# Gate phase of a hybrid GLA/SSD/PEER layer: part of the gate scaling on ScalarE, copies of the selection one step later, and another order of the last scalings

## The chip, the cores and the metric

One core of one Trainium2 chip runs the whole layer. The metric is the device time of one execution in microseconds (us), taken as the median over runs.

## The reference

The layer takes 512 tokens of width 1024. It normalises them, mixes them with a gated linear attention and a state-space mixer (the first 260 us, untouched here), and then applies a mixture of single-neuron experts. Only this last part matters:

```python
def peer_ffn(xn, w_query, sub_keys, u, v):   # T=512 tokens, H=8 heads, K=16, 128 keys
    q = (xt @ w_query).reshape(T, H, 2, PEER_HALF)
    s = jnp.einsum('thpd,hpkd->thpk', q, sub_keys)
    top_s, top_i = lax.top_k(s, K)
    cand_s = top_s[:, :, 0, :, None] + top_s[:, :, 1, None, :]     # 16 x 16 sums
    best_s, best_pos = lax.top_k(cand_s.reshape(T, H, K * K), K)
    expert_idx = i1 * 128 + i2        # the two key indices at best_pos
    gate = jax.nn.softmax(best_s, axis=-1)
    ...
    hid = gelu(xt . u[expert_idx]) * gate          # 128 experts per token
    return sum over the 128 of hid * v[expert_idx]
# y = rmsnorm(h + peer_ffn(rmsnorm(h)))
```

## The kernel before

For three of the four blocks of 128 tokens (384 tokens, TD) the kernel does not gather experts: it computes gelu(x . u) for all 16384 experts in 128 tiles of 128 experts, multiplies by a dense matrix of gates (zero where an expert was not picked), and multiplies by all of v. The fourth block is done by gathering rows with indirect DMAs, one expert per token at a time, spread over the rest of the program. The instructions of each engine run in the order in which the code issues them; there is no scheduler. The stages, in time:

- Queries, scores and top-16 searches, until 387 us. VectorE does the searches.
- Selection, 387 to 464 us. `select(t)` finds, for the block t, the two key indices of each of the 128 picks with long 16-bit VectorE operations on a tile `gat`. It reads copies of the index lists (tile `k`) that ScalarE writes; `ties(t)` queues four such copies (`piece`), and two of them are issued in each following U step. There are two buffers `k`, so those of block 2 take the one that `select(0)` reads. Meanwhile TensorE does U steps (`u_run`): a U step makes one tile of x . u in 8 parts (`u_part`) of 3 matmuls each. Every four parts need one half of a tile of u, split by ScalarE into a high part `uh` and by GpSimd, in this stage, into the low part `ul`. `spread` and `spread2` transpose the picks and write the key indices `i1s`, `i2s` and the gates `gs` (high part `gs[:, 0]`, low part `gs[:, 1]`, 16 bit).
- The gate phase, 464 to 655 us, is a loop over 48 units of 8 tokens. `gprep(u + 1)` builds on VectorE, for the next unit, the one-hot matrix `A` of the second key, the one-hot `eq` of the first key, and `B`, which is `eq` times the high gate part (`B[:, 0]`) and times the low one (`B[:, 1]`), 1024 elements per partition each. TensorE multiplies A and B of the unit (16 matmuls to `pg`). ScalarE writes the results of experts whose U tile is not there yet to `ring` and `stage`; VectorE multiplies the others into `ring`. `A` and `B` have two buffers, `eq` has one. Between two units TensorE does 5 or 6 parts of a U step. In this phase `ul` is done by VectorE. After a whole U step `keep` issues two gelu operations on ScalarE (`ring<-pm` and `gl<-pm`); the product with `gl` follows on VectorE in the next unit.
- The V stage, 660 to 1474 us: v streams through, TensorE is busy throughout.
- `final()`: the last products, residuals, means and scalings of the output.

The units' order of issue is short:

```python
act(stage[0][:, :, ...], p3[:, RS:, :], AF.Copy)   # gunit(u), ScalarE
gprep(u + 1)
release()                                          # product with gl
tt(ring[:, :n, w], p3[:, :n, :], ring[:, :n, w], OP.mult)
...
gunit(u)                                           # the loop over units
while done * NU < parts * (u + 1):
    u_part(done % 8)                               # uh and ul at parts 0 and 4
    done += 1
```

There are `parts` = 8 * (59 - 2 - 26) = 248 parts for 48 units, so 40 units have 5 and 8 have 6. Each unit's parts hold one or two uh copies (62 in all, at parts 0 and 4 of each U step) and 31 times the end of a U step with its gelu pair. Counted from this arithmetic: 11 units issue one uh copy alone, 6 one copy and then the gelu pair, 17 the gelu pair and then one copy, 6 two copies, 7 a copy, the pair and a copy, 1 the pair and then two copies.

Of the kernel before, what the change touches and what calls it, by code (L numbers as in the profile page):

```python
# [7 lines left out]
F32 = mybir.dt.float32  # L8
# [6 lines left out]
AF = mybir.ActivationFunctionType  # L15
OP = mybir.AluOpType
# [9 lines left out]
TD = GT * 128  # L26
# [3 lines left out]
def bc(ap, axis, n):  # L30
    shape = list(ap.shape)
    shape.insert(axis, n)
    ix = tuple([slice(None)] * axis + [None])
    return ap[ix].to_broadcast(shape)
# [29 lines left out]
class Layer:  # L64
# [25 lines left out]
    def act(self, out, in_, f, **k):  # L90
        return self.S.activation(out, in_, f, **k)  # L91
# [4 lines left out]
    def tt(self, out, x, y, op):  # L96
        return self.V.tensor_tensor(out, x, y, op=op)  # L97

    def stt(self, out, x, s, y, op0, op1, **k):
        return self.V.scalar_tensor_tensor(out, x, s, y, op0=op0, op1=op1, **k)  # L100
# [767 lines left out]
    def experts(self):  # L868
        tc, nc, a, V, T, G = self.tc, self.nc, self.a, self.V, self.T, self.G
        act, tt, stt, load = self.act, self.tt, self.stt, self.load  # L870
        ident, nh, nl = self.ident, self.nh, self.nl
        ctx = ExitStack()
        c = ctx.enter_context(tc.tile_pool(name="ex", bufs=1, reuse_waits="tile"))
# [3 lines left out]
        def pt():  # L877
            return self.ps.tile([128, 512], F32, name="pm", tag="pm", bufs=self.nbank)
# [9 lines left out]
        UT = 8  # L888
# [83 lines left out]
        def ties(t):  # L972
            x = (kp if t % 2 else self.kr).tile([128, 2, 8, 16, 16], F16, name="k8", tag="k8", bufs=1)
            for e in range(2):
                for g in (slice(0, 4), slice(4, 8)):
                    pieces.append((t, x[:, e, g], bc(tif[:, t, g, e, :], 3, 16)))
            TIE[t] = x
# [4 lines left out]
        def piece():  # L982
            t, o, i = pieces.pop(0)
            act(o, i, AF.Copy)

        def select(t):

            while any(p[0] == t for p in pieces):
                piece()
            ii = kp.tile([128, 2, 8, 16], F32, name="ii", bufs=2)  # L990
            for e in range(2):
                oh = c.tile([128, 8, 16, 16], F16, name="gat", tag="gat", bufs=3)
                tt(oh, bc(CF[0][:, e, t], 2, 16), bc(itj if e else its, 1, 8), OP.is_equal if e else OP.is_ge)
                tt(oh, oh, TIE[t][:, e], OP.mult)
                for n in (8, 4, 2):
                    tt(oh[:, :, 0:n, :], oh[:, :, 0:n, :], oh[:, :, n:2 * n, :], OP.add)
                tt(ii[:, e], oh[:, :, 0, :], oh[:, :, 1, :], OP.add)
            IX[t] = ii
# [9 lines left out]
        def gates2():  # L1008
            sm = kp.tile([128, 2, NT, 8], F32, name="sm")
            V.tensor_reduce(sm[:, 0], bs, axis=AX.X, op=OP.add)  # L1010
            V.reciprocal(sm[:, 1], sm[:, 0])
            tt(bs, bs, bc(sm[:, 1], 3, 16), OP.mult)
# [2 lines left out]
        i1s = c.tile([128, TD], F16, name="i1s")  # L1015
        i2s = c.tile([128, TD], F16, name="i2s")
        gs = c.tile([128, 2, TD], F16, name="gs")
        SC = float(2 ** 14)
        flat = lambda x: x.rearrange("p h k -> p (h k)")

# [2 lines left out]
        def spread(t):  # L1023
            ii, g = IX.pop(t), bs[:, t]
            p = pt()
            T.transpose(p[:, 0:128], flat(ii[:, 0]), ident)
            T.transpose(p[:, 128:256], flat(ii[:, 1]), ident)
            T.transpose(p[:, 256:384], flat(g), ident)
            act(gs[:, 0, t * 128:(t + 1) * 128], p[:, 256:384], AF.Copy, scale=SC)
            SPR[t] = p  # L1030

        def spread2(t):
            p = SPR.pop(t)
            s = slice(t * 128, (t + 1) * 128)
            V.tensor_copy(i2s[:, s], p[:, 128:256])
            V.tensor_copy(i1s[:, s], p[:, 0:128])
            stt(gs[:, 1, s], p[:, 256:384], SC, gs[:, 0, s], OP.mult, OP.subtract)

        nu, gtok = [NPU], [0]
        held, hold = [], [False]  # L1040
# [19 lines left out]
        def u_part(i, pool=False):  # L1060
            e = nu[0]
            if e >= NE:
                return
            if i == 0:
                up[0] = pt()
            self.rhs_part(up[0][:, :TD], tsd, not hold[0] and nu[0] < RS - 4)
            if i in PP and pieces:
                piece()
            if i == 7:
                keep(e, up[0])  # L1070
                nu[0] += 1

        def u_run(n):
            for _ in range(n):
                for i in range(8):
                    u_part(i)
# [23 lines left out]
        gates1()  # L1100
        select(0)
        gates2()
        u_run(2)
        ties(2)
        u_run(1)
        select(1)
        u_run(2)
        spread(0)
        ties(3)
        select(2)  # L1110
        u_run(2)
        spread(1)
        u_run(1)
        spread2(0)
        spread2(1)
        select(3)
        u_run(2)
        spread(2)
        u_run(5)
# [52 lines left out]
        def gprep(u):  # L1172

            if u >= NU:
                return
            w = slice(u * UT, u * UT + UT)
            two = lambda x: bc(x.rearrange("p (a t) -> p a t", t=2), 2, 128)
            A = gp.tile([128, UT // 2, 128, 2], F16, name="A", bufs=2)
            eq = gp.tile([128, UT // 2, 128, 2], F16, name="eq")
            B = gp.tile([128, 2, UT // 2, 128, 2], F16, name="B", bufs=2)  # L1180
            tt(A, bc(itx, 1, UT // 2), two(i2s[:, w]), OP.is_equal)
            tt(eq, bc(itx, 1, UT // 2), two(i1s[:, w]), OP.is_equal)
            for i in range(2):
                tt(B[:, i], eq, two(gs[:, i, w]), OP.mult)
            AB[u] = A, B

        def gunit(u):
# [76 lines left out]
        def final():  # L1264

            nv = lambda: c.tile([128, 4], F32, name="rs3", bufs=4)
            hf = [slice(0, 512), slice(512, 1024)]
            junk = [c.tile([128, D], F32, name="gat", tag="gat", bufs=3), vp.tile([128, D], F32, name=f"vr{NE % 4}", bufs=1)]
            v = [nv() for _ in range(4)]

            def products(t):
                s = slice(t * 128, t * 128 + 128)
                for n in range(2):
                    for e in (NE - 2, NE - 1):
                        self.mm3(pv[t][n], HT[e][0][:, s], HT[e][1][:, s], *vs.parts[2 * e + n], False, e == NE - 1)

            def residual(t, n):
                h = hs[t][:, hf[n]]
                stt(h, pv[t][n], 1.0 / SC, h, OP.mult, OP.add)
                square(t, n)  # L1280

            def square(t, n):
                act(junk[t % 2][:, hf[n]], hs[t][:, hf[n]], AF.Square, accum_out=v[t][:, n:n + 1])

            def weight(t, n, eng):
                eng.tensor_tensor(hs[t][:, hf[n]], hs[t][:, hf[n]], wf[:, hf[n]], op=OP.mult)

            def mean(t):
                V.tensor_scalar(v[t][:, 2:3], v[t][:, 0:1], EPS * D, None, op0=OP.add)
                V.tensor_scalar(v[t][:, 0:1], v[t][:, 1:2], v[t][:, 2:3], 1.0 / D, op0=OP.add, op1=OP.mult)  # L1290

            def power(t):
                G.tensor_tensor(v[t][:, 3:4], v[t][:, 0:1], self.mhalf, op=OP.pow)

            def scale(t, cols=slice(0, D)):
                stt(hs[t][:, cols], hs[t][:, cols], v[t][:, 3:4], wf[:, cols], OP.mult, OP.mult)

            square(3, 0)
            square(3, 1)
            mean(3)  # L1300
            power(3)
            for t in range(3):
                products(t)
            residual(0, 0)
            residual(0, 1)
            scale(3)
            load(self.out[3], hs[3])
            mean(0)
            power(0)
            residual(1, 0)  # L1310
            weight(1, 0, G)
            scale(0, hf[0])
            residual(1, 1)
            residual(2, 0)
            scale(0, hf[1])
            load(self.out[0], hs[0])
            residual(2, 1)
            mean(1)
            power(1)
            scale(1, hf[1])  # L1320
            mean(2)
            power(2)
            act(hs[1][:, hf[0]], hs[1][:, hf[0]], AF.Copy, scale=v[1][:, 3:4])
            load(self.out[1], hs[1])
            weight(2, 0, V)
            act(hs[2][:, hf[0]], hs[2][:, hf[0]], AF.Copy, scale=v[2][:, 3:4])
            self.S.dma_start(self.out[2][:, hf[0]], hs[2][:, hf[0]])
            scale(2, hf[1])
            load(self.out[2][:, hf[1]], hs[2][:, hf[1]])
# [152 lines left out]
```

## Time and profile before

| | |
|---|---|
| median of 3 runs (lowest to highest) | 1491.26 us (1488.55 to 1494.8) |
| profiled execution | 1490.63 us |
| its span of instructions | 1488.9 us, the rest (1.7 us) lies around it |
| busy, TensorE / VectorE / ScalarE / GpSimd | 98% / 79% / 43% / 31% of the span |
| chain that ended last | TensorE 79%, VectorE 14%, issue 3%, ScalarE 2%, DMA 2% |

The busy shares are averages over stages with different limits. The chain that ended last, read in order of time, tells which engine sets the pace where: VectorE all through the selection, TensorE and VectorE in turn in the gate phase, TensorE in the V stage. A busy TensorE is modelled from its matmuls, so a small gap there can hide.

### The profile page before, as it was taken

What the parts mean: (1) busy time and instruction counts of PE and PEld (TensorE: products, weight loads), DVE (VectorE), ACT (ScalarE), POOL (GpSimd) and SP (SyncE); (2) the same over time, 40 slices, a digit from 0 to 9 for tenths busy, and PEclk for the clock granted to TensorE, in tenths of its full rate; (3) what the DMA queues carried; (4) which work ended last, traced back from release to release, by engine and by line L of the source; (5) the groups of instructions that cost most, each with busy time, mean ns of one, the idle gap of its engine ahead of it and who ended that gap; (6) DMA issues with size and microseconds to landing.
All of it is one profiled execution on the core that took longest, in us unless ns stands there. A gap on an engine that the chain in (4) does not pass through costs nothing.

```text
span 1488.9 us, 22403 instructions
## 1 busy us (share of the span) xinstructions
PE 1453.5 (98%) x7896; PEld 1276.4 (86%) x7896; DVE 1174.1 (79%) x2476; ACT 636.2 (43%) x1208; POOL 456.2 (31%) x383
## 2 busy tenths in 40 slices
PE   7999999999999999999999999999999999999997
PEld 6787778888989998889999999999999998888886
DVE  6542664789999999988778778777788888888886
ACT  6335743433654544443333333333333333444444
POOL 2002404444574000003333333333333334333331
PEclk9999999999999999999999999999999999999999
DMA  5231224222334556679998898889898888888894
GB/s 190 85 127 58 71 72 156 89 91 91 100 114 158 145 157 167 180 226 341 321 322 311 307 328 310 312 315 324 309 346 306 310 300 289 293 302 294 299 326 171
DMA packets 148883, 335.56 MB, mean 225 GB/s; under 512 B 64657, under 2 KB 73889, under 8 KB 148641
## 3 DMA queue, kind: packets, MB, share of 16 engines
q1 hardware_dynamic: 58672, 186.06, 36.8%
q0 software_dynamic: 36864, 134.23, 25.1%
q10 hardware_dynamic: 53232, 13.83, 4.0%
q8 instruction: 62, 1.02, 0.3%
q14 instruction: 53, 0.43, 0.1%
HBM read 315.79 MB, written 18.28 MB: 224 GB/s over the span
## 4 chain that ended last, share of the span: by engine, by line
PE 79%; DVE 14%; issue 3%; ACT 2%; DMA 2%; POOL 0%; DVEq 0%; POOLq 0%; SPq 0%; ACTq 0%
PE pm L109 25%; PE pm L108 25%; PE pm L110 25%; DVE gat L97 4%; DVE B L97 1%; PE pg L1196 1%; DVE ul L104 1%; ACT b L91 1%; DVE eq L97 1%; DVE A L97 1%; DVE ring L97 1%; DMA ur<-in_uT 1%; PE pm L914 1%; ACT tp L91 0%; PE pm L275 0%
## 5 line engine op out<-in xcount | busy, mean ns | idle before, releaser
L108 PE MATMUL pm<-nT,uh 128*128 128x384 f32 (+1 forms) x1152 | 401.7, 349 | 0.9 <-ACT nT L91 0.5
L110 PE MATMUL pm<-nT,ul 128*128 128x384 f32 (+1 forms) x1152 | 396.6, 344 | 3.0 <-POOL ul L104 3.0
L109 PE MATMUL pm<-nT,uh 128*128 128x384 f32 (+1 forms) x1152 | 396.4, 344 | 0.5 <-DVE nT L97 0.5
L109 PE MATMUL pm<-vl,hh 128*128 128x512 f32 x765 | 300.6, 393 | 0.2 <-DVE vl L104 0.2
L110 PE MATMUL pm<-vh,hl 128*128 128x512 f32 x765 | 300.5, 393 | 0.0
L108 PE MATMUL pm<-vh,hh 128*128 128x512 f32 x765 | 298.9, 391 | 0.2 <-ACT vh L91 0.2
L1145 POOL DMA_INDIRECT gat<-in_u,idx x128 | 137.9, 1078 | 455.3 <-DVE gat L100 449.5
L91 ACT ACTIVATE uh<-ur 128x512 fp32r<-128x512 f32 x288 | 180.6, 629 | 201.0 <-PE pm L109 180.9
L108 PEld LDWEIGHTS pm<-nT,uh 128*128 128x128 f32 x1152 | 217.7, 189 | 25.6 <-ACT uh L91 1.0
L109 PEld LDWEIGHTS pm<-nT,uh 128*128 128x128 f32 x1152 | 217.6, 189 | 24.8 <-DVE nT L97 1.1
L110 PEld LDWEIGHTS pm<-nT,ul 128*128 128x128 f32 x1152 | 217.5, 189 | 10.5 <-POOL ul L104 4.7
L1145 POOL DMA_INDIRECT gat<-in_v,idx x128 | 146.9, 1148 | 253.4 <-DVE n2a L100 209.6
L91 ACT ACTIVATE vh<-vr 128x512 fp32r<-128x512 f32 x255 | 159.4, 626 | 136.8 <-PE pm L110 134.0
L104 DVE TENSOR_TENSOR vl<-vr,vh 128x512 fp32r<-128x512 f32 x255 | 175.0, 687 | 35.0 <-ACT vh L91 34.4
L104 DVE TENSOR_TENSOR ul<-ur,uh 128x512 fp32r<-128x512 f32 x202 | 138.1, 688 | 48.8 <-ACT uh L91 48.4
L100 DVE SCALAR_TENSOR_TENSOR n2a<-gat,dots,n2a 128x1024 f32<-128x1024 f32 x128 | 163.8, 1280 | 14.8 <-DMA gat<-in_v,idx 10.8
L110 PEld LDWEIGHTS pm<-vh,hl 128*128 128x128 f32 x765 | 143.7, 188 | 30.4
L100 DVE SCALAR_TENSOR_TENSOR gat<-gat,n2a 128x1024 f32<-128x1024 f32 x128 | 156.0, 1219 | 9.5 <-DMA gat<-in_u,idx 9.2
L108 PEld LDWEIGHTS pm<-vh,hh 128*128 128x128 f32 x765 | 143.9, 188 | 14.2 <-ACT vh L91 0.7
L109 PEld LDWEIGHTS pm<-vl,hh 128*128 128x128 f32 x765 | 143.9, 188 | 14.2 <-DVE vl L104 0.5
L104 POOL TENSOR_TENSOR ul<-ur,uh 128x512 fp32r<-128x512 f32 x86 | 124.9, 1461 | 98.6 <-ACT uh L91 95.7
L91 ACT ACTIVATE gl<-pm 128x384 f32<-128x384 f32 (+15 forms) x102 | 45.4, 445 | 220.1 <-PE pm L110 220.1
(252 smaller groups left out, 1694.5 us busy)
## 6 DMA issues: line engine op xcount, KB each, us to landing
ur<-in_uT SPq DMA_DIRECT2D x128, 512.0 KB, 5.7
vr<-in_v SPq DMA_DIRECT2D x128, 512.0 KB, 5.3
gd<-stage ACTq DMA_DIRECT2D x6, 2208.0 KB, 14.0
ring<-gd SPq DMA_DIRECT2D x69, 192.0 KB, 5.4
wraw<-in_w_in SPq DMA_DIRECT2D x23, 512.0 KB, 4.3
ur<-in_w_query SPq DMA_DIRECT2D x16, 512.0 KB, 3.7
b<-in_x SPq DMA_DIRECT2D x8, 512.0 KB, 3.6
wraw<-in_w_out SPq DMA_DIRECT2D x8, 512.0 KB, 3.9
```

The lines of the kernel that those rows point to most:

```text
L91: return self.S.activation(out, in_, f, **k)
L97: return self.V.tensor_tensor(out, x, y, op=op)
L100: return self.V.scalar_tensor_tensor(out, x, s, y, op0=op0, op1=op1, **k)
L104: (self.G if pool else self.V).tensor_tensor(lo, src, hi.bitcast(F32), op=OP.subtract)
L108: T.matmul(out, lhi, rhi, start=start, stop=False)
L109: T.matmul(out, lhi, rlo, start=False, stop=False)
L110: T.matmul(out, llo, rhi, start=False, stop=stop)
L914: T.matmul(p[:, t * 128:(t + 1) * 128], q[:, t * 128:(t + 1) * 128], skT[:, b, :], start=True, stop=True)
L1145: G.indirect_dma_start(out=r, out_offset=None, in_=src, in_offset=bass.IndirectOffsetOnAxis(ap=idx[:, k:k + 1], axis=0))
L1196: T.matmul(o, A[:, t // 2, :, t % 2], B[:, i, t // 2, :, t % 2], start=i == 0, stop=i == 1)
```

## The change

Three edits come together. In the gate phase, the product of `eq` and the low gate part is split: VectorE keeps the first four tokens of a unit (512 elements), and ScalarE does the other four, one ACTIVATE of 128 elements for each token, with the token's low gate as a scale read from memory. For this the low parts are also kept in 32 bits (`gl32`), so `spread2` writes them there and copies them to `gs`. In the selection the `ties` of blocks 2 and 3 are queued one U step later, and `spread`, `select` and `spread2` change places a little. In `final()` the product of the last block's first half with the norm's weights moves to GpSimd, and the mean and power of the last block stand ahead of the second half's scaling of the block before.

```diff
+        gl32 = c.tile([128, TD], F32, name="gl32")
...
-            stt(gs[:, 1, s], p[:, 256:384], SC, gs[:, 0, s], OP.mult, OP.subtract)
+            stt(gl32[:, s], p[:, 256:384], SC, gs[:, 0, s], OP.mult, OP.subtract)
+            V.tensor_copy(gs[:, 1, s], gl32[:, s])
...
         gates2()
-        u_run(2)
+        u_run(3)
         ties(2)
-        u_run(1)
         select(1)
         u_run(2)
         spread(0)
+        select(2)
+        u_run(1)
         ties(3)
-        select(2)
         u_run(2)
         spread(1)
-        u_run(1)
         spread2(0)
+        select(3)
         spread2(1)
-        select(3)
         u_run(2)
...
             tt(eq, bc(itx, 1, UT // 2), two(i1s[:, w]), OP.is_equal)
-            for i in range(2):
-                tt(B[:, i], eq, two(gs[:, i, w]), OP.mult)
+            tt(B[:, 0], eq, two(gs[:, 0, w]), OP.mult)
+            k = UT // 4
+            tt(B[:, 1, :k], eq[:, :k], two(gs[:, 1, w.start:w.start + UT // 2]), OP.mult)
+
+            for t in range(UT // 2, UT):
+                act(B[:, 1, t // 2, :, t % 2], eq[:, t // 2, :, t % 2], AF.Copy, scale=gl32[:, w.start + t:w.start + t + 1])
...
             residual(2, 0)
+            weight(2, 0, G)
             scale(0, hf[1])
             load(self.out[0], hs[0])
             residual(2, 1)
             mean(1)
             power(1)
-            scale(1, hf[1])
             mean(2)
             power(2)
+            scale(1, hf[1])
             act(hs[1][:, hf[0]], hs[1][:, hf[0]], AF.Copy, scale=v[1][:, 3:4])
             load(self.out[1], hs[1])
-            weight(2, 0, V)
```

On ScalarE, in the gate phase, this is the order before, over a little more than two units (`uh<-ur` is the copy that splits a half tile of u, `ring<-pm` and `gl<-pm` the gelu pair, `ring<-pg` and `stage<-pg` the results of a unit):

```order
L91 ACTIVATE ring<-pg 128x15x8
L91 ACTIVATE stage<-pg 128x69x8
L91 ACTIVATE uh<-ur_5846 128x512
L91 ACTIVATE ring<-pg 128x15x8
L91 ACTIVATE stage<-pg 128x69x8
L91 ACTIVATE ring<-pm 128x144
L91 ACTIVATE gl<-pm 128x240
L91 ACTIVATE uh<-ur_5912 128x512
```

And now, at the same units:

```order
L91 ACTIVATE ring<-pg 128x15x8
L91 ACTIVATE stage<-pg 128x69x8
L91 ACTIVATE B<-eq,gl_2226 128x128 x4
L91 ACTIVATE uh<-ur_5962 128x512
L91 ACTIVATE ring<-pg 128x15x8
L91 ACTIVATE stage<-pg 128x69x8
L91 ACTIVATE B<-eq,gl_2226 128x128 x4
L91 ACTIVATE ring<-pm 128x144
L91 ACTIVATE gl<-pm 128x240
L91 ACTIVATE uh<-ur_6032 128x512
```

The four scalings of the next unit stand between a unit's results and the copies uh (and gelu pairs) of that unit's parts.

On VectorE, at the same units, this is the order now (`ul<-ur,uh` is the low part of a half tile of u and reads uh):

```order
L97 TENSOR_TENSOR A<-itx,i2s 128x1024
L97 TENSOR_TENSOR eq<-itx,i1s 128x1024
L97 TENSOR_TENSOR B<-eq,gs 128x1024
L97 TENSOR_TENSOR B<-eq,gs 128x512
L97 TENSOR_TENSOR ring<-gl,ring 128x224
L97 TENSOR_TENSOR ring<-pg,ring 128x44x8
L104 TENSOR_TENSOR ul<-ur_5962,uh 128x512
L97 TENSOR_TENSOR A<-itx,i2s 128x1024
L97 TENSOR_TENSOR eq<-itx,i1s 128x1024
L97 TENSOR_TENSOR B<-eq,gs 128x1024
```

Before, the second B row had 128x1024 like the first; nothing else moved here, so ul still stands between the products of one unit and the A and eq of the next.

In the selection, ScalarE's order before, after the copies of block 1 (`k_3873` are the copies of block 2):

```order
L91 ACTIVATE ring<-pm 128x384
L91 ACTIVATE uh<-ur_3800 128x512 x2
L91 ACTIVATE ring<-pm 128x384
L91 ACTIVATE uh<-ur_3838 128x512
L91 ACTIVATE k_3873<-tif 128x1024
L91 ACTIVATE uh<-ur_3838 128x512
L91 ACTIVATE k_3873<-tif 128x1024
```

And now (`k_3910` are the copies of block 2):

```order
L91 ACTIVATE ring<-pm 128x384
L91 ACTIVATE uh<-ur_3801 128x512 x2
L91 ACTIVATE ring<-pm 128x384
L91 ACTIVATE uh<-ur_3839 128x512 x2
L91 ACTIVATE ring<-pm 128x384
L91 ACTIVATE uh<-ur_3875 128x512
L91 ACTIVATE k_3910<-tif 128x1024
```

One more U step's two uh copies and its gelu come ahead of the first copy.

## Rows read from the trace of the kernel before

**Rows 1.** Busy time by stretch: TensorE, its loads, VectorE, ScalarE, GpSimd; clock, DMA.

```profile
560.00:580.00 20.00, 19.25 (x160) 17.81 (x159) 19.64 (x37) 9.50 (x24) 0.00 (x0) 1.00 0.63 178
```

**Rows 2.** The chain that ended last, early gate phase: start, duration, what.

```profile
485.44 0.94 PE pg L1196 x16
489.03 0.94 PE pg L1196 x16
```

**Rows 3.** Timeline of VectorE, one unit: start, duration, operation.

```profile
576.62 0.68 DVE L97 TENSOR_TENSOR eq<-itx,i1s 128x1024 f16<-128x1024 f16 x1
577.34 1.29 DVE L97 TENSOR_TENSOR B<-eq,gs 128x1024 f16<-128x1024 f16 x2
578.54 0.39 DVE L97 TENSOR_TENSOR ring<-gl,ring 128x224 f32<-128x224 f32 x1
578.85 0.52 DVE L97 TENSOR_TENSOR ring<-pg,ring 128x352 f32<-128x352 f32 x1
579.28 0.68 DVE L104 TENSOR_TENSOR ul<-ur,uh 128x512 fp32r<-128x512 f32 x1
579.88 0.68 DVE L97 TENSOR_TENSOR A<-itx,i2s 128x1024 f16<-128x1024 f16 x1
580.48 0.68 DVE L97 TENSOR_TENSOR eq<-itx,i1s 128x1024 f16<-128x1024 f16 x1
```

**Rows 4.** Timeline of ScalarE, gate phase; in brackets idle before and what ended it.

```profile
570.29 0.63 ACT L91 ACTIVATE uh<-ur 128x512 fp32r<-128x512 f32 x1 [1.40 <-DMA ur<-in_uT]
...
573.60 0.30 ACT L91 ACTIVATE ring<-pm 128x160 f32<-128x160 f32 x1 [0.82 <-PE pm L110]
...
574.03 0.63 ACT L91 ACTIVATE uh<-ur 128x512 fp32r<-128x512 f32 x1
...
588.53 0.52 ACTq L1209 DMA_DIRECT2D gd<-stage  x1
```

**Rows 5.** Timeline of VectorE, gate phase: units 1 and 47, and two places between.

```profile
465.82 0.68 DVE L97 TENSOR_TENSOR eq<-itx,i1s 128x1024 f16<-128x1024 f16 x1
...
570.95 0.69 DVE L104 TENSOR_TENSOR ul<-ur,uh 128x512 fp32r<-128x512 f32 x1 [0.18 <-ACT uh L91]
...
607.55 1.22 DVE L100 SCALAR_TENSOR_TENSOR gat<-gat,n2a 128x1024 f32<-128x1024 f32 x1
...
650.25 0.68 DVE L97 TENSOR_TENSOR eq<-itx,i1s 128x1024 f16<-128x1024 f16 x1
```

**Rows 6.** ScalarE's groups by shape: count, busy us, mean ns of one, idle before.

```profile
L91 ACT ACTIVATE b<-pm,RT 128x128 f32<-128x128 f32 x32 | 9.0, 363 | 1.5 <-PE pm L573 1.5
...
L91 ACT ACTIVATE b<-b 128x512 f32<-128x512 f32 x8 | 5.0, 630 | 0.3
...
L91 ACT ACTIVATE b<-b,rs 128x512 f32<-128x512 f32 x3 | 2.1, 711 | 0.2 <-POOL rs L235 0.2
...
L91 ACT ACTIVATE dots<-dots 128x128 f32<-128x128 f32 x1 | 0.3, 312 | 3.2 <-DVE gat L100 3.2
```

**Rows 7.** Timeline of ScalarE, mixers: four operations of 128 elements in a row.

```profile
179.50 1.12 ACT L91 ACTIVATE b<-pm,RT 128x128 f32<-128x128 f32 x4
```

**Rows 8.** Waits, 465 to 655 us: in total, times, longest.

```profile
ACT uh L91 <- DMA ur<-in_uT: 3.8, 4, 1.5
```

**Rows 9.** Timelines of ScalarE and VectorE in the selection.

```profile
407.84 1.06 ACT L91 ACTIVATE k<-tif 128x1024 f16<-128x1024 f16 x1 [2.48 <-DVE gat L97]
...
394.23 0.43 DVE L97 TENSOR_TENSOR sc<-sc 128x512 f16<-128x512 f16 x1
...
399.68 4.40 DVE L97 TENSOR_TENSOR gat<-gat 128x1024 f16<-128x1024 f16 x3
...
407.84 1.48 DVE L97 TENSOR_TENSOR gat<-gat 128x1024 f16<-128x1024 f16 x3
```

**Rows 10.** Timeline of the tail: GpSimd's weight product, VectorE's scaling.

```profile
1478.56 1.30 POOL L1286 TENSOR_TENSOR ur<-ur,gat 128x512 f32<-128x512 f32 x1 [0.90 <-ACT vr L91]
...
1482.04 0.75 DVE L100 SCALAR_TENSOR_TENSOR ur<-ur,rs,gat 128x512 f32<-128x512 f32 x1 [0.66 <-POOL rs L1293]
```

## The prediction

> **What bounds the kernel now.** I read the chain that ended last first. It runs through VectorE in the selection, through TensorE and VectorE in turns in the gate phase, and through TensorE afterwards, so two of the three edits (selection, gate phase) sit where VectorE sets the pace, and the third in the tail, where everything is on the path. Next I read the gate phase in stretches: in its middle VectorE is busy 19.64 of 20 us, TensorE 19.25 and ScalarE only 9.50 [rows 1]. Early in the phase TensorE alone sets the pace: its units follow each other at 489.03 - 485.44 = 3.59 us when they hold five parts [rows 2]. Later a unit takes as long as VectorE's work for it. In the unit shown, from one `eq` to the next, that is 580.48 - 576.62 = 3.86 us [rows 3], with no idle time between the rows. From the `eq` of unit 1 to that of unit 47 the phase takes 650.25 - 465.82 = 184.43 us, 4.01 us for each of 46 units [rows 5].
>
> So the edit takes work from the engine that limits and gives it to one that is half idle. Whether that helps depends on where in ScalarE's queue the new work stands.
>
> **What VectorE is spared.** One product of 1024 elements becomes one of 512. A 1024-element one takes a slot of about 0.60 us (A starts at 579.88, eq at 580.48 [rows 3]); one of 512 elements of the same type lasts 0.43 instead of 0.68 us [rows 3, 9]. That is 0.26 us less a unit, 12.0 us over 46 units, on VectorE's own account.
>
> **What a scaling costs ScalarE.** No row shows the new operation itself: 128 elements, from SBUF, scaled by a pointer. Its parts are there. 128 elements without a pointer last 0.312 us; a scale read from memory takes 512 elements from 0.630 to 0.711, so 0.081 more [rows 6]. That gives 0.393 us for one. Four operations of 128 elements with a pointer, read from PSUM, take 1.12 us together and 0.363 each [rows 6, 7], so they start (1.12 - 0.363) / 3 = 0.252 apart and overlap by 0.11. With the same overlap the new ones start 0.28 to 0.29 apart, and four fill 1.16 us. The bounds are four times 0.252 = 1.01 below, because a PSUM source is quicker, and four times 0.393 = 1.57 above, if they don't overlap at all. I take 1.16, since a scaling of the same kind (the 0.711 row) shows the pointer's price directly.
>
> The trace's nearest sequence, the one from PSUM, starts its operations 0.252 us apart [rows 7]. The Trainium skill (ScalarE: Activation LUTs, What ACT_TABLE_LOAD costs) states 186 ns plus 0.833 ns an element, about 93 ns more for each pointer operand, and an overlap of about 93 ns. By the row alone four scalings would fill 1.01 us and the sum below would be 1494.4; by the page they would fill an estimated 1.17 us, and the sum would be about 1502. The page speaks against cutting this product into pieces of one token.
>
> **The new loop.** The four scalings of unit u+1 wait for its `eq`, and ScalarE works in order. That order is seen at 407.84, where a copy `k` kept ScalarE idle for 2.48 us [rows 9] with the split of the next half tile right behind it. In the changed order the copies `uh` of unit u's parts, and any gelu pair ahead of them, stand behind the scalings. On VectorE `ul` waits for `uh`, and `A` and `eq` of unit u+2 stand behind `ul`. So each unit closes a chain from `eq` to `eq` through both engines, which the old order did not have, since `uh` did not wait for VectorE's `eq`:
> - `eq` until the operation that uses it starts: 577.34 - 576.62 = 0.72 us [rows 3].
> - four scalings: 1.16.
> - `uh` until `ul` starts: 570.95 - 570.29 = 0.66 [rows 4, 5].
> - `ul` until A starts 0.60, A until eq starts 0.60 [rows 3].
>
> Together 3.74 us, for units with one copy and no gelu pair ahead of it (11 + 6 = 17 units). A gelu pair ahead of the copy adds 574.03 - 573.60 = 0.43 [rows 4]: 4.17 for 17 units. A second copy adds one more `ul`, 0.60: 4.34 for 6 units. Copy, pair, copy adds 0.43 and one copy's slot, 0.63 - 0.11 = 0.52: 4.69 for 7 units. Pair and two copies: 4.77, once. The sum over 48 units is 63.6 + 70.9 + 26.0 + 32.8 + 4.8 = 198.1 us. Between the two `eq` of [rows 5] the last two units (a pair and a copy, and a copy with the pair behind it, 4.17 and 3.74) fall out: 190.2 us.
>
> Added to that, inside the same chain:
> - one product of a gathered row on VectorE, 1.2 us [rows 5], which is in the old 184.43 too.
> - the `stage` write-out, issued five times in these units from ScalarE's queue, 0.52 us each [rows 4], now ahead of `uh`. Between nothing (if it is issued while the scalings run) and 2.6; I take 1.5.
> - waits of `uh` for the loads of u, 3.8 us in all before [rows 8]. They can shrink, because a slower loop gives the loads more time, or stay; I take 2, between 0 and 3.8.
>
> The gate phase comes to 190.2 + 1.2 + 1.5 + 2.0 = 194.9, against 184.4: **10.5 us more**. TensorE then waits about 0.4 us a unit for B; its own 3.59 [rows 2] stays below every loop.
>
> **The selection.** Three more conversions of 128 elements on VectorE's chain are each shorter than the 0.43 of 512 elements [rows 9]; I take 0.7 us for the three, 1.3 at most, nothing at least. The moved copies free ScalarE of waits like the 2.48 us one [rows 9], so that TensorE's U steps end earlier. But VectorE's chain ends last here, and it runs slower beside GpSimd's `ul`: the same three additions take 4.40 us beside it and 1.48 alone, at the time of that wait [rows 9]. Fewer waits for ScalarE put more `ul` beside those additions, and fewer beside the last ones, since the number of `ul` is the same. I take 0 for this, with -3 to +5.8 as its bounds (one group fewer, or two groups more, at 2.9).
>
> **The tail.** The second half's scaling (0.75 us [rows 10]) leaves the chain to the last mean, and a weight product leaves VectorE. In exchange GpSimd does that product (1.30 us on this engine [rows 10]) ahead of the power that the scaling waits for. Between -0.75 and 1.30 - 0.75 = +0.55; I take -0.7, since the product has time from the moment its square is done.
>
> **Sum.** The changes add 10.5 + 0.7 - 0.7 = 10.5 us. The profiled execution took 1490.63 us, 0.63 below the median, so 1501.1 on its scale and **1501.8, say 1502**, on the median's.
>
> **Rivals.**
> - The gain that VectorE's account promises: if ScalarE is always early enough, the 12.0 us leave the path except where TensorE's 3.59 us already binds; I put that at 8 us, less 0 to 1 for the other edits: 1483. For it speaks ScalarE's half-empty time [rows 1]; against it, that the time is empty in the wrong place: `uh` stands behind a wait for VectorE. It decides from where the loop is shorter than before, that is when four scalings fill less than 1.16 - 10.5 / 46 = 0.93 us, below my lower bound of 1.01.
> - The loop is there, but the scalings follow each other as in [rows 7], at 0.252: 46 times 0.16 less, 7.4 us, so 1494.4: no change that can be told.
> - The selection suffers too: two groups of additions come to lie beside GpSimd's work, 5.8 us [rows 9], on top of the loop: 1507.6.
>
> **How the numbers follow.** About 0.5%, 7.5 us, is what a measurement of this kernel can tell from no change. The loop as priced gets 0.62, the loop with the dearer selection 0.10: both slower by over 0.5% (0.72). The cheaper scalings, or a loop partly hidden, get 0.20: within 0.5%. The gain gets 0.08. The likeliest is 1502. Upward, the selection's 5.8 us and the upper ends of the write-outs (1.1) and load waits (1.8) reach 1510, leaving out unoverlapped scalings (1.57 instead of 1.16, 19 us), which I don't believe. Downward, the cheaper scalings and the selection's -3 reach 1491, leaving out the gain. So 1491 to 1510, with about 0.15 outside.
>
> **What would show it.** In the changed profile: one B scaling lasts 0.39 us and four fill 1.16; VectorE, 98% busy in mid phase now [rows 1], falls to about 87%, idle ahead of `ul`, waiting for `uh` on ScalarE, for some 20 us in all where it was nearly nothing; ScalarE idles ahead of the first of the four, waiting for `eq`; `eq` to `eq` over 46 units is 195 us, and TensorE's gap ahead of `pg` is put down to B. The k copies' waits for `gat` in the selection disappear. What would make it wrong: VectorE idle only for TensorE, units at 3.6 us, and `uh` starting right after its half tile is free; scalings 0.2 us apart; or a selection shorter by more than 3 us.

## The result and the profile after

The changed kernel takes 1508.15 us (median of 3 runs, 1506.29 to 1510.52) against 1491.26. The ratio is 1.0115, with a 95% interval from 1.009 to 1.0139: it is slower, by 1.15%. The profiled execution took 1506.29 us, with a span of 1504.5.

The page of the changed kernel, its busy time and its chain that ended last:

```profile
PE 1460.9 (97%) x7896; PEld 1277.2 (85%) x7896; DVE 1164.5 (77%) x2478; ACT 688.1 (46%) x1400; POOL 458.4 (30%) x384
...
PE 46%; issue 20%; DVE 15%; POOL 9%; ACT 8%; DMA 2%; POOLq 0%; ACTq 0%; DVEq 0%; SPq 0%
```

ScalarE has come into the chain with 8%, where it had 2%. TensorE's share fell from 79% to 46%, although it is nearly as busy as before: from 686 to 1079 us the chain now runs through the gathers of rows of u (GpSimd's 9% and most of the 20% of issue) and comes back to TensorE at the standstill that is shown below. Where the 15.6 us between the two spans lie is read stage by stage, between the same instructions of both traces:

| stretch | before | after | difference |
|---|---|---|---|
| start to `eq` of unit 1 (selection included) | 465.82 | 467.00 | +1.2 |
| `eq` of unit 1 to that of unit 47 | 184.43 | 195.52 | +11.1 |
| from there to the first `hh` | 11.36 | 11.10 | -0.3 |
| first `hh` (ScalarE's copy of one tile of hidden values) to the first square of the tail (V stage) | 810.63 | 814.89 | +4.3 |
| from there to the end | 16.66 | 15.99 | -0.7 |

The start of unit 1's `eq`, and the tile views of `B` and `eq` (duration lowest, median and highest in ns, first and last start):

```profile
467.00 0.68 DVE L97 TENSOR_TENSOR eq<-itx,i1s 128x1024 f16<-128x1024 f16 x1
```

```profile
L91 ACT ACTIVATE B<-eq,gl x192: 417/425/450, 465.3 to 664.2; 128x128 f16<-128x128 f16 x192
...
L97 DVE TENSOR_TENSOR eq<-itx,i1s x48: 679/684/693, 464.6 to 662.5; 128x1024 f16<-128x1024 f16 x48
```

The last `eq` starts at 662.5, so 46 units take 195.5 us. In the same 20 us as [rows 1], VectorE is now busy for 17.32 us, 87%, and TensorE for 18.71:

```profile
560.00:580.00 20.00, 18.71 (x155) 17.02 (x154) 17.32 (x33) 13.83 (x41) 0.00 (x0) 1.00 0.69 191
```

The waits of 460 to 680 us (in total, times, longest) name who waits for whom:

```profile
ACT B L91 <- DVE eq L97: 54.5, 47, 2.5
DVE ul L104 <- ACT uh L91: 25.9, 42, 2.2
PEld L1201 <- DVE B L97: 21.2, 43, 1.2
PE pg L1201 <- DVE B L97: 12.4, 26, 1.8
```

ScalarE, in front of the first of four scalings, waits for `eq` in nearly every unit; VectorE waits for `uh` 42 times, 39 of them between the two `eq` of the table (22.6 us there, 3.6 before); TensorE waits for B. ScalarE's timeline shows how the two waits hang together:

```profile
577.76 1.32 ACT L91 ACTIVATE B<-eq,gl 128x128 f16<-128x128 f16 x4 [0.94 <-DVE eq L97]
578.95 0.29 ACT L91 ACTIVATE ring<-pm 128x168 f32<-128x168 f32 x1
579.14 0.33 ACT L91 ACTIVATE gl<-pm 128x216 f32<-128x216 f32 x1
579.37 0.62 ACT L91 ACTIVATE uh<-ur 128x512 fp32r<-128x512 f32 x1
...
582.01 1.32 ACT L91 ACTIVATE B<-eq,gl 128x128 f16<-128x128 f16 x4 [1.34 <-DVE eq L97]
583.20 0.61 ACT L91 ACTIVATE uh<-ur 128x512 fp32r<-128x512 f32 x1
```

And VectorE's at the same place:

```profile
576.99 0.68 DVE L97 TENSOR_TENSOR eq<-itx,i1s 128x1024 f16<-128x1024 f16 x1
...
580.02 0.69 DVE L104 TENSOR_TENSOR ul<-ur,uh 128x512 fp32r<-128x512 f32 x1 [0.87 <-ACT uh L91]
580.63 0.69 DVE L97 TENSOR_TENSOR A<-itx,i2s 128x1024 f16<-128x1024 f16 x1
581.24 0.68 DVE L97 TENSOR_TENSOR eq<-itx,i1s 128x1024 f16<-128x1024 f16 x1
...
586.01 0.69 DVE L97 TENSOR_TENSOR eq<-itx,i1s 128x1024 f16<-128x1024 f16 x1
...
589.83 0.69 DVE L97 TENSOR_TENSOR eq<-itx,i1s 128x1024 f16<-128x1024 f16 x1
```

One turn of the loop, read across both engines: eq 576.99, first scaling 577.76, gelu pair 578.95, uh 579.37, ul 580.02, A 580.63, next eq 581.24. That is 4.25 us for a unit with a pair ahead of its copy. The next unit has a copy, a pair and a copy (581.24 to 586.01, 4.77), the one after it a single copy (3.82). Before, a unit at this place took 3.86 [rows 3]. Taken over all 46 units, nearly the whole loss lies in one kind: the 16 units with a pair ahead of their only copy take 4.32 us in the mean, where the same units took 3.71 before, which is 9.7 of the 11.1 us. The 11 units with one copy alone take 3.82 in both kernels: there the loop is just as long as VectorE's own work was.

In the selection the copy `k` at 407.81 no longer waits (2.48 us at this place in [rows 9]), but the three additions at the same time now take 4.40 us where they took 1.48; GpSimd's `ul` runs beside them from 404.75 to 411.68, where GpSimd stood idle before from 406.72 to 409.49. The waits of the copies for `gat` moved rather than went: before, one of 2.48 and one of 2.79 us, now one of 5.13 ahead of the copy at 425.66:

```profile
407.81 1.04 ACT L91 ACTIVATE k<-tif 128x1024 f16<-128x1024 f16 x1
```

```profile
407.43 4.40 DVE L97 TENSOR_TENSOR gat<-gat 128x1024 f16<-128x1024 f16 x3
```

In the tail, GpSimd's extra product and VectorE's last scaling, to be held against [rows 10]:

```profile
1496.80 1.27 POOL L1291 TENSOR_TENSOR gat<-gat 128x512 f32<-128x512 f32 x1 [0.71 <-ACT gat L91]
```

```profile
1499.27 0.75 DVE L100 SCALAR_TENSOR_TENSOR gat<-gat,rs 128x512 f32<-128x512 f32 x1
```

The V stage, in which nothing was changed, lost 4.3 us. Its first `hh` copies show no loss at first and one later. Two stretches of four tiles each, on ScalarE:

```profile
903.27 0.51 ACT L91 ACTIVATE hh<-ring 128x384 fp32r<-128x384 f32 x1
...
936.55 0.51 ACT L91 ACTIVATE hh<-ring 128x384 fp32r<-128x384 f32 x1
...
1137.93 0.51 ACT L91 ACTIVATE hh<-ring 128x384 fp32r<-128x384 f32 x1
...
1171.69 0.51 ACT L91 ACTIVATE hh<-ring 128x384 fp32r<-128x384 f32 x1
```

The early four take 33.28 us (8.32 a tile), the late four 33.76 (8.44 a tile). Between them lies a standstill of TensorE, at the place where the gathers turn from rows of u to rows of v (waits of TensorE and its loads, 1055 to 1105 us):

```profile
PEld pm L109 <- DVE vl L104: 0.9, 1, 0.9
...
PE pm L109 <- DVE vl L104: 0.5, 1, 0.5
```

So two questions went to the chip: whether the loop makes the gate phase's 11.1 us, and what the V stage's 4.3 us are.

### The profile page after: what moved, and what is told of

Same layout as the page of the kernel before. It is cut to its first block, busy times and chain, and to the rows that moved or that the text cites. A ratio compares the mean times of both kernels' runs of the same rounds, so it can differ in the third digit from the quotient of the medians.

```text
span 1504.5 us, 22602 instructions
## 1 busy us (share of the span) xinstructions
PE 1460.9 (97%) x7896; PEld 1277.2 (85%) x7896; DVE 1164.5 (77%) x2478; ACT 688.1 (46%) x1400; POOL 458.4 (30%) x384
## 4 chain that ended last, share of the span: by engine, by line
PE 46%; issue 20%; DVE 15%; POOL 9%; ACT 8%; DMA 2%; POOLq 0%; ACTq 0%; DVEq 0%; SPq 0%
PE pm L109 14%; PE pm L108 14%; PE pm L110 14%; POOL gat L1146 9%; DVE gat L97 4%; ACT B L91 3%; DVE ul L104 2%; DVE A L97 2%; DVE eq L97 2%; ACT uh L91 2%; PE pm L914 1%; ACT b L91 1%; DMA gat<-in_u,idx 1%; DMA ur<-in_uT 1%; ACT tp L91 0%
```

## Experiments

The theory is the loop: scalings that wait for `eq` stand ahead of `uh`, `ul` waits for `uh`, and the next `eq` stands behind `ul`. The rivals are that the scalings cost by their amount, wherever they stand, and that the selection carries a good part of the loss. In the table, "46 units" goes from `eq` to `eq`; for e3 and e8, which move `eq`, it goes from `A` to `A`, which is 184.5 for the kernel before. The ratio is that to the kernel before in the same series (medians 1490.39, 1490.37 and 1491.28 for e1 to e4, e5 to e8, e9 and e10).

| | median (us) | ratio, interval | 46 units | V stage |
|---|---|---|---|---|
| before, first series | 1491.26 | | 184.4 | 810.6 |
| after, first series | 1508.15 | 1.0115 [1.009, 1.0139] | 195.5 | 814.9 |
| e1, gate edit alone | 1507.34 | 1.0118 [1.009, 1.0146] | 195.6 | 815.9 |
| e2, the rest alone | 1491.41 | 0.9996 [0.998, 1.0013] | 184.0 | 814.1 |
| e3, eq one unit earlier | 1480.04 | 0.9938 [0.9922, 0.9953] | 172.0 | 810.9 |
| e4, constant scale | 1492.27 | 1.0025 [1.0001, 1.0048] | 183.6 | 811.8 |
| e5, two tokens | 1498.41 | 1.0046 [1.0029, 1.0063] | 181.1 | 819.7 |
| e6, scalings behind uh | 1494.85 | 1.0021 [0.9997, 1.0044] | 179.5 | 810.6 |
| e7, one gl buffer | 1503.99 | 1.0107 [1.0072, 1.0143] | 194.9 | 814.3 |
| e8, before with eq earlier | 1484.21 | 0.9957 [0.9943, 0.9971] | 178.4 | 810.6 |
| e9, no load of n2a | 1508.61 | 1.0111 [1.0075, 1.0148] | 195.2 | 819.9 |
| e10, after again | 1511.65 | 1.0138 [1.0121, 1.0155] | 195.5 | 819.2 |

The last two columns are from each kernel's profiled execution, the median from all its runs. That matters in e4, e5, e6 and e9, whose runs lie up to some 10 us apart, about as much as the two paces of the V stage (below) make. That it is the V stage in the runs without a profile is likely and not shown.

**e1 and e2, the change in two halves.** e1 is the kernel before with the gate phase's edit (and `gl32`); e2 is the changed kernel without it (changed kernel to e2):

```diff
...
-            tt(B[:, 0], eq, two(gs[:, 0, w]), OP.mult)
-            k = UT // 4
...
+            for i in range(2):
+                tt(B[:, i], eq, two(gs[:, i, w]), OP.mult)
...
```

> The gate edit alone (with the 32-bit copy of the low gates it needs); selection and last scalings as before. Theory of the loop (eq, four scalings, uh, ul, A, eq in a ring): from the eq of unit 1 to that of unit 47 195 us as in the changed kernel (184.4 before), so about 11 us slower than before by the gate phase alone and 12 with the conversions. Rival, that the selection's new order carries a good part of the 17 us: gate phase still 195, but the whole only 8 to 10 us slower. If the extra 4 us of the V stage come with the later gate phase they are here too (15 to 16 us slower); if they are chance, not.

> The selection's new order and the last scalings alone; VectorE does both low halves as before. Theory of the loop: gate phase 184 to 185 us, selection 1 us longer, tail 0.7 shorter, the whole within 1.5 us of before. Rival, that the selection carries a good part: 3 to 6 us slower than before.

e1 gives the whole loss: 195.6 us in the gate phase, and 815.9 in the V stage, which its expectation had named as the sign that this part, too, comes with the later gate phase and is not chance. e2 can't be told from the kernel before by its median of ten runs. So the loss belongs to the gate phase's edit; that the selection carries a good part of it is refuted.

**e3, `eq` built one unit earlier.** The scalings keep their place, size and number; only what they wait for is ready earlier (two buffers for `eq`, and one for `gl` instead of two, to make room).

```diff
...
+            EQ[u] = gp.tile([128, UT // 2, 128, 2], F16, name="eq", bufs=2)
...
-            tt(eq, bc(itx, 1, UT // 2), two(i1s[:, w]), OP.is_equal)
...
             AB[u] = A, B
+            eqprep(u + 1)
...
```

> The changed kernel with eq built one unit earlier (a second buffer for eq, one buffer instead of two for gl), so that the scalings wait for no eq of the same unit; the scalings, their number and their place in ScalarE's order stay. Theory of the loop: the ring is cut, ScalarE no longer waits for eq, VectorE keeps its relief of 0.26 us a unit, and the 46 units take 172 to 178 us: 17 to 23 us less than the changed kernel, 5 to 10 less than before. Rival, that the mere amount of ScalarE work or its memory traffic is what costs: the 46 units stay near 195 us.

Its waits, 460 to 680 us, with none of ScalarE for `eq` among the long ones:

```profile
ACT ring L91 <- PE pg L1208: 31.2, 40, 1.3
DVE ul L104 <- ACT uh L91: 12.7, 18, 2.6
```

46 units take 172.0 us, 23.5 less than in the changed kernel, with the same 192 scalings on ScalarE. The median of 1480.04 us is 0.6% below the kernel before. That the scalings cost by their amount is refuted.

**e4, a constant in place of the pointer.** The scale is 0.5 for all four tokens, so the low parts of half the tokens are other numbers.

```diff
-                act(B[:, 1, t // 2, :, t % 2], eq[:, t // 2, :, t % 2], AF.Copy, scale=gl32[:, w.start + t:w.start + t + 1])
+                act(B[:, 1, t // 2, :, t % 2], eq[:, t // 2, :, t % 2], AF.Copy, scale=0.5)
```

> The changed kernel with a constant in place of the token's gate as scale, so the low gate parts are wrong for half the tokens; the order is unchanged. It tells the price of the pointer. Theory of the loop: a scaling starts 0.20 to 0.22 us after the one before instead of 0.30, four fill 0.8 to 0.85 instead of 1.19, and each of 46 units is 0.35 us shorter: 195.5 falls to 179 to 181 us, the whole to about 1492. Rival, that the units are not bound by the scalings: no change by more than 3 us.

```profile
L91 ACT ACTIVATE B<-eq x192: 326/334/358, 466.3 to 653.0; 128x128 f16<-128x128 f16 x192
```

One scaling lasts 334 ns instead of 425, and the phase becomes 11.9 us shorter, 0.26 a unit: the direction that the loop asks for, and less than was expected (0.35 a unit, 179 to 181 us). Scalings shorter by 91 ns each thus bring the median to within 2 us of the kernel before; four of the ten runs, at 1498.70 to 1501.58, lie some 10 us above the other six. The Trainium skill (ScalarE: Activation LUTs, What ACT_TABLE_LOAD costs) gives about 93 ns for a pointer operand, which these two medians confirm; its 186 ns plus 0.833 ns an element would make 293 ns without the pointer, an estimate that the 334 here exceeds.

**e5 and e6, less and later.** e5 leaves two tokens on ScalarE (`k = 3`, and the loop over `t` from 6). e6 leaves four, but issues them behind the first `uh` of the unit's parts:

```diff
...
                 u_part(done % 8)
+                if done % 4 == 0:
+                    scales()
                 done += 1
...
```

> The changed kernel with two tokens of a unit on ScalarE instead of four (VectorE's half product grows to 768 elements). Loop theory: two scalings fill 0.298 + 0.425 = 0.72 us instead of 1.32, so each loop from eq to eq shrinks by 0.60 us (4.25 to 3.65, 4.77 to 4.17, 3.82 to 3.22). That is below VectorE's own work for a unit (4.01 us before, less about 0.13), which binds again: from eq of unit 1 to eq of unit 47 178 to 184 us, total 1485 to 1492. Rival, that each token on ScalarE costs the phase a share of its own (port or memory contention): half of the 11 us stays, 190 us and about 1500.

> The changed kernel with the four scalings of unit u+1 issued on ScalarE behind the first copy uh of unit u's parts instead of ahead of it; every instruction and size is the same, only this place differs. Loop theory: the first uh and a gelu pair ahead of it wait for no eq any more, so the loop is open except in the 14 units with a second copy; VectorE's saving of 0.26 us a unit comes through and the gate phase falls to 172 to 181 us from 195.5, total 1480 to 1490. Danger that it shows too: TensorE waits for B in units where the scalings now end late. Rival, that the scalings cost by their amount of work wherever they stand: 193 to 196 us, 1505 to 1510.

The gate phases came as the loop has it, 181.1 and 179.5 us. In e6 only the place in ScalarE's order differs from the changed kernel, and 16 us are gone. ScalarE's timeline of e6 has no wait for `eq` there:

```profile
573.56 0.63 ACT L91 ACTIVATE uh<-ur 128x512 fp32r<-128x512 f32 x1
574.08 1.31 ACT L91 ACTIVATE B<-eq,gl 128x128 f16<-128x128 f16 x4
```

The totals missed what was expected (1485 to 1492 and 1480 to 1490): most runs of both were 6 to 13 us longer than the shortest, 1488.76 and 1485.18. In e5's profile the excess lies in the V stage, 819.7 us against 810.6.

**e7, a control.**

> The changed kernel with one buffer for gl instead of two, as e3 had it, and nothing else: a control. Loop theory: gl has time, the gate phase stays at 195 to 197 us and the total at 1506 to 1511. Rival, that e3 gained by this buffer: under 1500. It also is a second look at the V stage: if the 4 us that the V stage lost in the changed kernel belong to the change, its length from the first hh to the first square of the tail is 814 to 816 us here too; if they come and go from run to run, 811 to 812 is as likely.

194.9 us and a loss like the changed kernel's (the median came 2 us below what was expected): the buffer that e3 gave up explains nothing of its gain. The V stage took 814.3 us, in the range that stood for a loss that belongs to the change.

**e8, `eq` earlier in the kernel before.** The same edit as e3's, with all products on VectorE.

> The kernel before (all products of B on VectorE) with eq built one unit ahead, as in e3. Loop theory: without scalings on ScalarE nothing ahead of uh waits for eq, and VectorE has the same work as before, so nothing changes: eq to eq over 46 units 183 to 186 us, 1489 to 1494. Rival, that the earlier eq is worth 20 us by itself, whatever ScalarE does: 1475 to 1485, and e3's gain over the kernel before would then owe nothing to the moved scalings.

Here my theory missed: the kernel gained 6 us, and 46 units take 178.4 instead of 184.5. VectorE's timeline of e8 shows why:

```profile
573.45 0.69 DVE L97 TENSOR_TENSOR A<-itx,i2s 128x1024 f16<-128x1024 f16 x1
574.05 1.29 DVE L97 TENSOR_TENSOR B<-eq,gs 128x1024 f16<-128x1024 f16 x2
575.26 0.69 DVE L97 TENSOR_TENSOR eq<-itx,i1s 128x1024 f16<-128x1024 f16 x1
...
579.00 0.69 DVE L97 TENSOR_TENSOR eq<-itx,i1s 128x1024 f16<-128x1024 f16 x1
```

The product B now starts 0.60 us behind A, which it does not read; before, it stood directly behind the `eq` that it reads and started 0.72 behind it [rows 3]. A unit takes 575.26 to 579.00, 3.74 instead of 3.86 us. 46 times 0.12 is 5.5 of the 6.1 us. So of e3's 12.5 us over the kernel before, 6.1 belong to the earlier `eq` by itself and 6.4 to the products moved to ScalarE. That is what VectorE's account of 12.0 us was worth here once the loop was open; from there on TensorE sets the pace, busy for all of 520 to 580 us in e3 (the columns are those of [rows 1]):

```profile
520.00:580.00 60.00, 60.00 (x516) 57.46 (x514) 57.31 (x114) 48.47 (x141) 0.00 (x0) 1.00 0.61 173
```

**e9 and e10, the V stage.** e9 is the changed kernel without the load that VectorE waits for at the turn of the gathers; e10 is the changed kernel unaltered.

```diff
-                    load(acc[0], self.hd[GT])
+                    V.memset(acc[0], 0.0)
```

> The changed kernel without the load of the residual into n2a in the V stage (n2a starts from zero by a VectorE memset, so the fourth block's output lacks its residual). It asks about the part of the loss that lies outside the gate phase: in the changed kernel VectorE waited 2.9 us for that load, TensorE then stood for 1.4 us for the low part vl, and from there on TensorE took 8.44 instead of 8.32 us a tile until the U steps end. Theory that the standstill sets off the slower tiles: without it the V stage, from the first hh to the first square of the tail, takes 810.5 to 811.7 us instead of 814.9 and the total falls by 3 to 5 us against the changed kernel run beside it, to 1502 to 1504. Rival, that the slower tiles come from something else or from run to run: 814 to 820 us, and the same total as the changed kernel within 2 us. The gate phase is 195.5 us either way.

> The changed kernel once more, unaltered, beside e9. Expected as first measured: 1506 to 1510 us, gate phase 195.5 us from eq to eq over 46 units, V stage 814 to 816 us with the standstill at the load of n2a. If the V stage varies from run to run, 811 is possible.

e9 leaves out the fourth block's residual with that load. The standstill was gone, and the theory still fell: its V stage took 819.9 us. Its four runs were 1504.18, 1504.48, 1512.73 and 1513.99. e10 came out above what was expected, 1511.65 us with a V stage of 819.2. In it the four tiles of the two stretches shown for the changed kernel are the other way round:

```profile
908.24 0.52 ACT L91 ACTIVATE hh<-ring 128x384 fp32r<-128x384 f32 x1
...
942.00 0.51 ACT L91 ACTIVATE hh<-ring 128x384 fp32r<-128x384 f32 x1
...
1145.56 0.51 ACT L91 ACTIVATE hh<-ring 128x384 fp32r<-128x384 f32 x1
...
1178.84 0.51 ACT L91 ACTIVATE hh<-ring 128x384 fp32r<-128x384 f32 x1
```

33.76 us before the standstill, 33.28 behind it. So there are two paces, 8.32 and 8.44 us a tile, and the slower one needs no standstill (e9); at a standstill the pace can change from either to the other.

## Why the prediction was right

The forecast was 1502 us, between 1491 and 1510, slower; measured were 1508.15. By the steps of the prediction:

- **The loop** is there as it was put: scalings waiting for `eq`, `uh` behind them, `ul` waiting for `uh`, `eq` behind `ul`. Shown by the waits above and by e3 and e6, which open it in two ways without taking a scaling away.
- **Its length.** Units of three kinds were put at 4.17, 4.69 and 3.74 us; they took 4.25, 4.77 and 3.82. The 0.08 too few lie in the scalings, from the first one to what follows them 1.19 us instead of 1.16 (577.76 to 578.95), and in `eq` to the first of them, 0.77 instead of 0.72. The prediction priced this loop for every unit; it did not ask in which units the loop is longer than VectorE's old work, and there (a pair ahead of the only copy) lies nearly all of the loss.
- **The scaling itself** lasts 425 ns, not 393, but four start (1.32 - 0.425) / 3 = 0.298 us apart, where 0.28 to 0.29 was taken. What follows starts while the fourth still runs, so the spacing decides and not the duration. The Trainium skill's numbers (ScalarE: Activation LUTs, What ACT_TABLE_LOAD costs) made an estimated 386 ns and 0.293 us: too low for the one, right for the other.
- **The phase** was put at 194.9 us and took 195.5, in part by chance: 46 times 0.08 is 3.7 us more than priced, and the allowances for write-outs and load waits, 3.5 us together, were not needed in that size.
- **VectorE's idle time** ahead of `ul` was put at some 20 us and was 22.6 between the two `eq` (25.9 in the stretch shown); its busy share in mid phase at 87%, as measured.
- **Selection and tail.** +0.7 was forecast for the selection. All that lies ahead of the first `eq` of the table gained +1.2, with the dearer additions at 407.43 and cheaper ones elsewhere (3.42 us at 419.42 instead of 4.39 at 414.74); e2, with both, can't be told from no change. That the copies' waits for `gat` would disappear was wrong: 5.13 us stayed, against 5.27 before. The tail gave back 0.7 as forecast.
- **The rivals.** The gain to 1483 did not come, since `uh` stood behind the wait. Scalings 0.252 us apart are refuted by the 0.298. The dearer selection, which would have come out at 1507.6 and so nearest to the median, is refuted by e1 and e2.
- **What was missing** is a term for the V stage. The prediction had TensorE's pace there as given; it cost 4.3 us in the profiled execution, 0.9 of it at the stage's beginning and the rest from the standstill on. With the loop it makes 15.4 of the profiled execution's 15.6 us, where 10.5 were forecast. That the median still lies within the range, 2 us under its upper end, is luck: the range went up to 1510 for a dearer selection, write-outs and load waits, none of which came in that size, and the V stage filled their place.

## What to carry to other kernels

When work is moved to an engine that is half idle, read what stands behind it in that engine's order, and follow whether something there leads back to the engine that feeds it: a chain of 3.8 to 4.8 us through both engines took the place of 3.9 us on one, and the freed 0.26 us a unit went under. Such a loop is opened by having its input ready one step ahead (e3) or by placing the waiting work behind what nobody should wait for (e6); the work itself need not shrink. And compare stage by stage: e6's gate phase is 5 us shorter than before, and its median says "same".

## What the runs showed of the hardware that was not expected

TensorE runs the mix of u and v products in the V stage at one of two paces, and the profile shows no idle time between its matmuls at either. The stretch from 850 to 1000 us, in which both kernels do the same, of the changed kernel in its first profile and in e10:

```profile
850.00:1000.00 150.00, 150.00 (x759) 135.81 (x759) 119.76 (x205) 55.74 (x108) 50.50 (x47) 1.00 0.89 316
```

```profile
850.00:1000.00 150.00, 150.00 (x748) 135.22 (x748) 116.72 (x200) 54.19 (x105) 50.10 (x47) 1.00 0.89 315
```

TensorE is busy all the time in both, the granted clock is 1.00 (2.4 GHz) in both, and the one does 759 matmuls, the other 748. No single gap makes the difference: in four tiles of the changed kernel at either pace (from 903.27 and from 1150 us) no two successive matmuls start more than 0.24 us apart. Away from the beginning of the stage and from the turn of the gathers, eight tiles usually take 66.56 or 67.52 us in all twelve profiles; a single `hh` that starts early or late moves such a stretch by up to 1.8. e5 and e9 held the slower pace from the first tiles to the end of the U steps, about 9 us more than the kernel before; the changed kernel, e1, e2 and e7 went over to it at or soon after a standstill at that turn, e10 came back from it there, and the others, e4 with a shorter standstill of 0.7 us among them, kept the faster one. Of all these, e2 (whose profiled run, 1496.57 us, is the slowest of its ten) and e5 show the slower pace without the changed kernel's longer gate phase.

The change has no instruction in the V stage, yet its loss there is not the chance of one execution. At the V stage's length before, the profiled execution of the changed kernel would have taken 1502.0 us. All seven runs of the changed kernel and all four of e1 lie at least 3.6 us above that, and of e7's four two (1502.42 and 1502.90) come near it, while of the 55 runs of the kernel before only five lie above 1495. So a loss beyond the gate phase comes regularly with the gate phase's edit; by what way is not shown. Which pace an execution starts with, and why it changes at a standstill, stays open too: no run here set it at will.

The second is VectorE's price for reading what the instruction directly ahead has just written, 0.12 us a time (0.72 against 0.60 us from start to start, e8), 48 times in the gate phase.
